# Attention of a diffusion block: value products in four column tiles, reciprocals spread by DMA, both heads' scores in float32r, inverse roots from Ln and Exp, GpSimd takes sums

## The chip, the cores and the metric

The kernel runs on one core of a Trainium2 chip. A core has TensorE (PE, matrix products; the loading of its stationary operand is shown as PEld), VectorE (DVE), ScalarE (ACT), GpSimd (POOL) and SyncE (SP, which here only issues DMA transfers). The on-chip memory SBUF has 128 partitions; TensorE writes its sums into PSUM, eight banks of 128 x 512 float32. Each engine runs its own instructions in order, and semaphores order the engines among themselves. The metric is device microseconds of one execution, as the median of several runs.

## The reference

Two layers of a diffusion transformer on 512 tokens of width 1024 with 256 tokens of context. Layer 0 mixes tokens by a Fourier transform and a long convolution, layer 1 by attention with low-rank queries, keys and values. Both end with a gated convolutional feed-forward. The change touches layer 1's attention and its output projection:

```python
def _rms_norm(x, g):
    y = x32 * lax.rsqrt(jnp.mean(x32 * x32, axis=-1, keepdims=True) + EPS)
    return (y * _f32(g)).astype(x.dtype)
...
q = (_rms_norm(a_q, q_a_norm) @ w_uq).reshape(B, L, MLA_HEADS, QK_HEAD_DIM)   # 16 heads of 64 + 32
q = _rms_norm(q, q_norm)                       # then the rotation of the last 32
...
k = _rms_norm(jnp.concatenate([k_nope, k_pe], axis=-1), k_norm)               # 512 + 256 keys
...
s = jnp.einsum('bqhd,bkhd->bhqk', qblk, k) * scale
p = jax.nn.softmax(s, axis=-1)
o = jnp.einsum('bhqk,bkhv->bqhv', p, v)        # value heads of 64
...
yx = o @ mla_w_o[j]
x = x + g1 * yx
```

## The kernel before

All weights and activations of the large products are kept as a float32r pair, a high part (a copy by ScalarE, `hi`, L240) and a residual (a subtraction by VectorE, `lo`, L245). `mm3` (L263 to L267) makes a product of three float32r products: high by high, high by residual, residual by high. Some products are plain float32 instead.

Attention runs over eight pairs of heads, `p` = 0 to 7. The heads of a pair are `a` = 0 and 1. Keys lie in six tiles `j` of 128 (four of tokens, two of context); the 512 queries are the free dimension. The scores therefore stand as keys x queries. The work of each pair is cut into small named steps, and the text `ORDER` (L36 to L66) lists all steps of all pairs in the order in which they are written out; TensorE, VectorE, ScalarE and GpSimd then run their own instructions in exactly that order. SyncE (the engine SP, not the step of that name) isn't held to it, but its queue is in order too. A step `SC13.5` is the step SC with a = 1, j = 3 of pair 5. The steps:

- QT, TB: products for the queries and their rotation; UK: key products, into the PSUM tile "k2"; SQ, RD, KSQ, KS: squares and their sums; TX: the rotation. KH and KL: high part and residual of the keys in SBUF. Only head 0 has a residual; head 1's keys are float32, in two alternating buffers.
- RT: the inverse roots of 20 columns of sums of squares, by `rsqrt` (L269 to L285): a start value from integer operations, then three Newton steps, 11 VectorE instructions, after two that form the means.
- U: scales the queries by these roots (four ScalarE instructions a head); TR: four transposes; QC and QL: high part and residual of the queries, QL for head 0 only.
- SC: a score tile 128 x 512. Head 0 by `mm3`, head 1 as one float32 product (L2019). EV: ScalarE copies it to SBUF, scaled by the key's root.
- MA, MB, MC, MD: VectorE's maximum over the six tiles. AR: GpSimd's maximum over the 128 partitions. SU: VectorE subtracts it, three tiles at a time. EX: ScalarE's Exp, three tiles at a time.
- PW: value products of one key tile (L2072), two matrix products with 64 columns of values each, one a head, in two column tiles of the array, into one "pv" bank. ON: the sums of the exponentials (L2083), four products with 32 columns of ones, in four column tiles, into the other "pv" bank. "pv" has two buffers.
- RC: reciprocal of the sums, 128 x 256, each row of which stands 32 times. TO: ScalarE copies the value products out of PSUM. SP: two TensorE products with a mask (L2098) that bring the reciprocals to the value rows' layout. DV: VectorE's product of both. OH, OL: high part and residual of the attention's output.
- VP, VE: the values of all heads, made on the way of the first pairs. WA/WD and XA/XD: splits of the query weights and of the output projection's weights, into the buffers "wh" and "wl" (three each, as "wr" for raw weights). WO m k: the output projection's block m of 128 columns with pair k's output.

Blocks 0 and 1 of the output projection are formed by WO within ORDER, in the attention's PSUM. The function `res_proj` does the other six, in two halves of 256 tokens; block 2's weights come split from the attention, those of the other blocks are loaded and split as they come (block 2's and 3's again for the second half). The residual is spilled to DRAM during attention and read back behind it.

Of the kernel before, what the change touches and what calls it, by code (L numbers as in the profile page):

```python
# [48 lines left out]
EV12.3 SC13.3 SU11.2 EX10.2 SC14.3 SC15.3 RT.4 EX11.2 ON0.2 PW0.2 EV13.3 ON1.2 MB0.3 KH0.4 PW1.2 U0.4 MC0.3 ON2.2 KL0.4 PW2.2 KH1.4 MD0.3 ON3.2 EV14.3
ON4.2 AR0.3 ON5.2 U1.4 MA1.3 PW3.2 PW4.2 EV15.3 RC.2 PW5.2 TR0.4 TO.2 SU00.3 QT.5 QC0.4 QL0.4 EX00.3 MB1.3 TR1.4 MC1.3 SQ.5 SP.2 TB.5 QC1.4 SC00.4  # L50
XA0.7 DV.2 SC01.4 TX.5 EV00.4 SC02.4 RD.5 EV01.4 SC03.4 MD1.3 EV02.4 SC04.4 SU01.3 EV03.4 AR1.3 UK.5 EV04.4 OH.2 SC10.4 XD0.7 KSQ.5 SC05.4 EV10.4
SC11.4 MA0.4 EV05.4 SC12.4 EX01.3 SU10.3 SC13.4 EV11.4 KS.5 SU11.3 EV12.4 EX10.3 SC14.4 RT.5 SC15.4 EX11.3 PW0.3 ON0.3 EV13.4 ON1.3 MB0.4 U0.5 PW1.3
MC0.4 ON2.3 OL.2 KH0.5 PW2.3 KH1.5 MD0.4 ON3.3 ON4.3 KL0.5 EV14.4 AR0.4 ON5.3 U1.5 PW3.3 MA1.4 PW4.3 EV15.4 RC.3 PW5.3 TR0.5 TO.3 SU00.4 QT.6 QC0.5
QL0.5 EX00.4 MB1.4 TR1.5 MC1.4 SC00.5 SQ.6 TB.6 SP.3 QC1.5 EV00.5 RD.6 SC01.5 SC02.5 TX.6 EV01.5 DV.3 SC03.5 EV02.5 MD1.4 SC04.5 OH.3 SU01.4 SC05.5
AR1.4 EV03.5 UK.6 EV04.5 EV05.5 OL.3 SC10.5 KSQ.6 SC11.5 MA0.5 EX01.4 SC12.5 SU10.4 EV10.5 KS.6 EV11.5 EV12.5 SU11.4 SC13.5 EX10.4 SC14.5 RT.6 SC15.5
EX11.4 ON0.4 ON1.4 EV13.5 PW0.4 MB0.5 EV14.5 ON2.4 U1.6 MC0.5 ON3.4 ON4.4 MA1.5 PW1.4 U0.6 PW2.4 MD0.5 KH0.6 MB1.5 ON5.4 AR0.5 PW3.4 KH1.6 RC.4 PW4.4
EV15.5 TR1.6 KL0.6 PW5.4 QC1.6 SU00.5 TR0.6 TO.4 QT.7 QC0.6 MC1.5 EX00.5 QL0.6 MD1.5 SC00.6 SU01.5 AR1.5 SQ.7 SP.4 EV00.6 SC01.6 XA1.7 TB.7 SC02.6
EV01.6 DV.4 SC03.6 EV02.6 TX.7 SC10.6 RD.7 EV03.6 SC04.6 EX01.5 SU10.5 UK.7 EV10.6 SC05.6 SU11.5 EV04.6 SC11.6 EV05.6 SC12.6 KSQ.7 XD1.7 SC13.6 EV11.6
EV12.6 MA0.6 KS.7 EX10.5 MB0.6 SC14.6 EX11.5 RT.7 SC15.6 ON0.5 EV13.6 ON1.5 PW0.5 EV14.6 MC0.6 U0.7 ON2.5 MA1.6 PW1.5 U1.7 PW2.5 MD0.6 MB1.6 ON3.5
AR0.6 KH0.7 ON4.5 ON5.5 KH1.7 KL0.7 PW3.5 EV15.6 RC.5 PW4.5 OH.4 PW5.5 XA2.7 SU00.6 TR0.7 TO.5 TR1.7 QC0.7 SP.5 QC1.7 QL0.7 WO00.7 EX00.6 MC1.6 SC00.7  # L60
SU01.6 SC01.7 EV00.7 SC02.7 EV01.7 SC03.7 MD1.6 EX01.6 SC04.7 OL.4 AR1.6 WO10.7 DV.5 EV02.7 WO01.7 EV03.7 XD2.7 SC10.7 EV04.7 OH.5 SC11.7 MA0.7 EV10.7
SC05.7 EV11.7 SU10.6 SC12.7 EV05.7 SC13.7 EV12.7 SU11.6 WO02.7 EX10.6 SC14.7 EV13.7 WO11.7 MB0.7 EX11.6 WO03.7 MC0.7 SC15.7 OL.5 EV14.7 WO12.7 MD0.7
EV15.7 ON0.6 MA1.7 AR0.7 PW0.6 ON1.6 MB1.7 ON2.6 PW1.6 MC1.7 ON3.6 MD1.7 ON4.6 SU00.7 PW2.6 AR1.7 ON5.6 PW3.6 RC.6 EX00.7 PW4.6 PW5.6 SU10.7 WO13.7
TO.6 WO04.7 SU01.7 EX10.7 WO14.7 SP.6 SU11.7 PW0.7 EX01.7 ON0.7 ON1.7 DV.6 EX11.7 PW1.7 ON2.7 PW2.7 OH.6 ON3.7 OL.6 ON4.7 ON5.7 PW3.7 RC.7 PW4.7 PW5.7
SP.7 TO.7 WO15.7 DV.7 WO05.7 OH.7 WO16.7 OL.7 WO06.7 WO07.7 WO17.7
"""  # L66
SPLIT = (0,)
# [119 lines left out]
class Builder:  # L187
# [1031 lines left out]
    def res_proj(self, i, sec, src_h, src_l, nk, wsrc, x, parts, hook=None, keep=None, ready=0, pre=None, there=False, ahead=None):  # L1219
# [7 lines left out]
        ws = dict(ahead or {})  # L1227

# [13 lines left out]
        for stage, part in enumerate(parts):  # L1242
            for j, m in enumerate(second if stage else range(KD)):
# [4 lines left out]
                if not (stage and (m >= KD - 3 or m < kept)) and not first and (stage or m not in ws):  # L1248
                    ws[m] = load(m)
                wh, wl = ws.get(m, (None, None))  # L1250
                ps = pre if first else self.mm()
                for k in range(0 if first else nk):
                    w = slice(128 * k, 128 * k + 128)
                    for a, n in part:
                        self.mm3(ps[:, a : a + n], wh[:, w], wl[:, w], src_h[k][:, a : a + n], src_l[k][:, a : a + n], k == 0, k == nk - 1)
# [467 lines left out]
    def attention(self, x, hh, hl, steps, aw):  # L1723
# [12 lines left out]

        K = [[self.t(pa, [P, TW], F32R if a in SPLIT else F32, f"K{a}{q}") for q in range(2)] for a in range(2)]
        keys = lambda p, a: K[a] if a in SPLIT else [K[a][p % 2]]
        tabm, tabx = self.t(pa, [P, 4, 192], F32, "tabm"), self.t(pa, [P, 4, 64], F32, "tabx")
        ssp = self.t(pa, [P, 20], F32, "ssp")  # L1740
        msk = self.t(pa, [P, 418], F32, "msk")
        rot, ksel, fan, ones = msk[0:64, 0:128], msk[:, 128:130], (msk[:, 130:258], msk[:, 258:386]), msk[:, 386:418]
# [53 lines left out]
        with self.tc.manual_schedule(engines={ENG.PE, ENG.DVE, ENG.Activation, ENG.Pool}):  # L1796
# [98 lines left out]
            rt, prot = MS(), [S1(), S1()]  # L1895
# [13 lines left out]
            def rotary_out():  # L1909
                v.memset(ssp, EPS)  # L1910
                v.tensor_scalar(ssp[:, 8:20].rearrange("p (a b) -> p a b", b=2), rt[:, 0:6].rearrange("p (a o) -> p a o", o=1).to_broadcast([P, 6, 2]),
                                1.0 / 96, EPS, op0=ALU.mult, op1=ALU.add)
                for a in range(2):
                    rows = slice(64, 128) if a == 0 else slice(0, 64)
                    for ps, (o, m) in zip(prot, sg):
                        self.hi(K[a][0][rows, o : o + m], ps[rows, :m])
                        if a in SPLIT:
                            self.lo(K[a][1][rows, o : o + m], ps[rows, :m], K[a][0][rows, o : o + m])
                    if a not in SPLIT:
                        nc.gpsimd.tensor_copy(K[a][1][rows, :], K[a][0][rows, :])  # L1920

# [46 lines left out]
            def KH(c, p, a):  # L1968
                rows = slice(0, 64) if a == 0 else slice(64, 128)
                self.hi(keys(p, a)[0][rows, :], c.k[rows, :TW])  # L1970
# [5 lines left out]
            def KS(c, p):  # L1976
                c.rt = MS()
                for j, t0 in enumerate(tok):
                    nc.tensor.matmul(c.rt[:, 2 * j : 2 * j + 2], c.ks[:, t0 : t0 + 128], ksel, start=True, stop=True)

            def RT(c, p):

                s = self.t(self.sm, [P, 24], F32, "nrm_s", 4)
                v.tensor_scalar(s[:, 0:8], c.s[:, 0:8], 1.0 / 96, EPS, op0=ALU.mult, op1=ALU.add)
                v.scalar_tensor_tensor(s[:, 8:20], c.rt[:, 0:12], 1.0 / 96, ssp[:, 8:20], op0=ALU.mult, op1=ALU.add)
                c.r = self.t(pq, [P, 24], F32, "rks", 3)
                self.rsqrt(self.sm, s, 20, c.r)

            def U(c, p, a):
                for t_ in range(4):  # L1990
                    q = c.t[:, t_, 128 * a : 128 * a + 128]
                    nc.scalar.activation(q, q, AF.Copy, scale=c.r[:, 2 * t_ + a : 2 * t_ + a + 1])
# [8 lines left out]
            def QC(c, p, a):  # L2001
                if not hasattr(c, "qT"):
                    c.qT, c.S, c.m, c.P, c.Z, c.ps = {}, {}, {}, None, None, {}
                q = self.t(pq, [P, T], F32R if a in SPLIT else F32, f"q{a}")
# [8 lines left out]
            def SC(c, p, a, j):  # L2013
                ps = c.ps[a, j] = S1()
                k_, q = [t_[:, tok[j] : tok[j] + 128] for t_ in keys(p, a)], c.qT[a]
                if a in SPLIT:
                    self.mm3(ps, *k_, *q, True, True)
                else:
# [672 lines left out]
```

## Time and profile before

| | |
|---|---|
| median of three runs | 1561.67 us (1561.05 to 1565.24) |
| the profiled execution | 1566.02 us |
| its span in the trace | 1564.3 us |
| mean granted TensorE clock | 0.991 |
| the listed order in that span, about | 954 to 1172 us |
| output projection behind it, about | 1172 to 1210 us |

The profile is one execution. A timeline row has start, duration, engine, line of the kernel, operation, result <- operands by the program's names, shape and count; matrix products are pipelined, so that durations overlap and the distance between starts is what one costs. A row of costly groups has busy time and mean duration in ns, then the idle time ahead of the group and what ended it. A row by windows has busy microseconds and instructions of each engine in a stretch, the granted clock and the DMA engines' share. A row of transfers has the issuing queue, count, KB each and the median time from issue to landing.

### The profile page before, as it was taken

The page shows a single profiled execution, that of the slowest core. Times are in us where ns is not written, and L with a number is a line of the kernel's source. Part 1 is how long each engine was busy: PE and PEld are TensorE (multiplying, and loading weights), DVE is VectorE, ACT ScalarE, POOL GpSimd, SP SyncE. Part 2 cuts the span into 40 slices and gives each one's busy share as a digit, 9 for nine tenths or more (in the row PEclk, how much of TensorE's full clock was granted, in tenths as well). Part 3 has the DMA queues.
Part 4 walks back from the last instruction along what each step waited for, and adds up shares of the span by engine and source line. Part 5 has one row for each costly group of instructions (what it writes and reads, how often), then busy time and mean ns, then how long its engine had stood idle before and what let it go on. Part 6 is the DMA issues. An engine that isn't in the chain of part 4 may idle for free.

```text
span 1564.3 us, 24106 instructions
## 1 busy us (share of the span) xinstructions
PE 1519.6 (97%) x9192; PEld 1310.9 (84%) x9192; DVE 1284.0 (82%) x2197; ACT 748.5 (48%) x1130; POOL 255.8 (16%) x407
## 2 busy tenths in 40 slices
PE   7999998999999999999999999999999999999998
PEld 5687888888999999999889887656559999989997
DVE  5788969968997997886769767899877999878884
ACT  4451224426543444443334337988855555434442
POOL 0013125201011112111111000112130021212100
PEclk9999998999999999999999999999999999999999
DMA  9336512536267778788686711000044365656543
GB/s 351 114 108 205 184 67 68 175 136 210 74 168 191 190 189 199 186 213 218 175 210 192 268 53 44 14 14 15 14 117 133 95 164 160 157 142 160 143 111 105
DMA packets 84513, 224.17 MB, mean 143 GB/s; under 512 B 10283, under 2 KB 16621, under 8 KB 83373
## 3 DMA queue, kind: packets, MB, share of 16 engines
q1 hardware_dynamic: 60205, 161.72, 31.3%
q0 software_dynamic: 24192, 60.91, 18.8%
q8 instruction: 72, 1.18, 0.3%
q14 instruction: 44, 0.36, 0.1%
HBM read 201.01 MB, written 21.58 MB: 142 GB/s over the span
## 4 chain that ended last, share of the span: by engine, by line
PE 72%; DVE 13%; DMA 8%; issue 3%; ACT 3%; POOL 1%; SPq 0%; ACTq 0%; DVEq 0%; POOLq 0%
PE mm L265 16%; PE mm L266 16%; PE mm L267 16%; DMA sb<-wmodT 3%; DVE junk L347 3%; PE pv L2072 3%; PE s L2019 3%; PE ms L265 3%; PE ms L266 3%; PE ms L267 3%; DVE wl L245 2%; DMA sb<-w_up 2%; PE pv L2083 2%; ACT wh L240 1%; PE k L266 1%
## 5 line engine op out<-in xcount | busy, mean ns | idle before, releaser
L240 ACT ACTIVATE wh<-wr 128x1024 fp32r<-128x1024 f32 (+3 forms) x182 | 158.1, 878 | 199.4 <-PE mm L266 120.8
L265 PE MATMUL mm<-hh,wh 128*128 128x512 f32 (+3 forms) x704 | 232.5, 330 | 2.1 <-DVE xr L1343 1.5
L266 PE MATMUL mm<-hl,wh 128*128 128x512 f32 (+3 forms) x704 | 230.4, 327 | 2.4 <-DVE hl L424 2.3
L267 PE MATMUL mm<-hh,wl 128*128 128x512 f32 (+3 forms) x704 | 229.8, 326 | 2.3 <-DVE wl L245 2.3
L245 DVE TENSOR_TENSOR wl<-wr,wh 128x1024 fp32r<-128x1024 f32 (+3 forms) x182 | 184.4, 1018 | 16.4 <-ACT wh L240 16.0
L265 PEld LDWEIGHTS mm<-hh,wh 128*128 128x128 f32 x704 | 134.7, 191 | 14.3 <-issue 4.7
L266 PEld LDWEIGHTS mm<-hl,wh 128*128 128x128 f32 x704 | 134.5, 191 | 11.8 <-DVE hl L424 3.3
L267 PEld LDWEIGHTS mm<-hh,wl 128*128 128x128 f32 x704 | 134.0, 190 | 12.1 <-DVE wl L245 4.5
L347 DVE SCALAR_TENSOR_TENSOR junk<-wr,sb 128x1024 bf16<-128x1024 f32 x96 | 117.2, 1221 | 4.2 <-DMA wr<-wmodT 4.1
L265 PE MATMUL ms<-hh,wh 128*128 128x386 f32 (+2 forms) x240 | 76.3, 318 | 1.1 <-DVE fg L1527 1.1
L266 PE MATMUL ms<-hl,wh 128*128 128x386 f32 (+2 forms) x240 | 76.3, 318 | 0.0
L267 PE MATMUL ms<-hh,wl 128*128 128x386 f32 (+2 forms) x240 | 76.3, 318 | 0.0
L267 PE MATMUL mm<-x,wl 128*128 128x512 f32 (+1 forms) x224 | 75.9, 339 | 0.3 <-DVE wl L245 0.3
L266 PE MATMUL mm<-x,wh 128*128 128x512 f32 (+1 forms) x224 | 76.0, 339 | 0.0
L265 PE MATMUL mm<-x,wh 128*128 128x512 f32 (+1 forms) x224 | 76.0, 340 | 0.0
L265 PE MATMUL mm<-ah,wh 128*128 128x512 f32 x176 | 69.7, 396 | 0.0
L266 PE MATMUL mm<-al,wh 128*128 128x512 f32 x176 | 69.7, 396 | 0.0
L267 PE MATMUL mm<-ah,wl 128*128 128x512 f32 x176 | 69.7, 396 | 0.0
L2027 ACT ACTIVATE S<-s,rks 128x512 f32<-128x512 f32 x96 | 62.8, 686 | 3.8 <-PE s L267 1.9
L2044 POOL PARTITION_ALL_REDUCE mx<-mx x16 | 38.2, 2385 | 158.6 <-DVE mx L2041 140.7
L2278 POOL DMA_DIRECT2D sum<-w_up x40 | 23.4, 601 | 234.8 <-DVE wl L245 160.4
L240 ACT ACTIVATE wh<-sum 128x1024 fp32r<-128x1024 f32 x40 | 42.3, 1058 | 36.0 <-PE mm L266 14.5
(514 smaller groups left out, 4521.2 us busy)
## 6 DMA issues: line engine op xcount, KB each, us to landing
wr<-wmodT SPq DMA_DIRECT2D x48, 512.0 KB, 4.1
wr<-w_up SPq DMA_DIRECT2D x48, 512.0 KB, 4.0
sum<-w_up POOLq DMA_DIRECT2D x80, 256.0 KB, 4.4
sb<-wmodT SPq DMA_DIRECT2D x32, 512.0 KB, 4.8
xs<-delta POOLq DMA_DIRECT2D x32, 386.0 KB, 6.5
wr<-w_dn SPq DMA_DIRECT2D x48, 256.0 KB, 3.8
sa<-w_up POOLq DMA_DIRECT2D x40, 256.0 KB, 4.3
sb<-w_up POOLq DMA_DIRECT2D x40, 256.0 KB, 5.1
```

Of the source, the lines that this page charges most:

```text
L240: self.nc.scalar.activation(dst, src, AF.Copy)
L245: (eng or self.nc.vector).tensor_tensor(dst, src, hi.bitcast(F32), op=ALU.subtract)
L265: mmul(out, wh, xh, start=start, stop=False)
L266: mmul(out, wh, xl, start=False, stop=False)
L267: mmul(out, wl, xh, start=False, stop=stop)
L347: nc.vector.scalar_tensor_tensor(junk, raw, 1.0, self.sb[j], op0=ALU.mult, op1=ALU.mult, accum_out=acc)
L2019: nc.tensor.matmul(ps, k_[0], q[0], start=True, stop=True)
L2027: nc.scalar.activation(c.S[a][j // 3][:, j % 3, :], c.ps[a, j], AF.Copy, scale=c.r[:, g : g + 1])
L2044: nc.gpsimd.partition_all_reduce(c.m[a][:, 1, :], c.m[a][:, 0, :], P, bass.bass_isa.ReduceOp.max)
L2072: nc.tensor.matmul(c.P[64 * a : 64 * a + 64, :], V[:, j, o : o + 64], c.S[a][j // 3][:, j % 3, :], start=c.np == 0, stop=c.np == 5, tile_p ...
L2083: nc.tensor.matmul(c.Z[o : o + 32, 0:256], ones, c.S[a][j // 3][:, j % 3, 256 * h : 256 * h + 256], start=c.nz == 0, stop=c.nz == 5, tile_ ...
L2278: nc.gpsimd.dma_start(t_[:, 512:1024], g[:, 0:512])
```

## The change

1. PW: four products of 32 value columns in four column tiles, instead of two of 64. In the new ORDER, PW and ON stand together more often.
2. Head 1's scores by `mm3` as well. So there are KL1 and QL1; keys have one buffer (high part, residual) for each head.
3. RC's input is first copied (ZC) and sent over DRAM (ZA, two transfers: four rows of 256 out, 128 x 8 in), so that the reciprocal works on 128 x 8; ZB sends it back to DRAM and ZD's two transfers read it as rows spread over 64 partitions each. TO and SP go; DV multiplies the value products in PSUM directly.
4. RT in three steps: NA (the two means' instructions), NB (ScalarE: Ln, then Exp with the factor -0.5), RT (one Newton step, three instructions). One table load stands ahead of ORDER.
5. GpSimd subtracts the maximum for one key tile in six (SV; the second SU has two tiles) and forms OL.
6. U of head 0 is one VectorE product with a broadcast operand. MB and MC become one operation of two tiles. A head's scores stand in one buffer of six tiles (four buffers) instead of two of three (eight).
7. Block 2 of the output projection is done in ORDER too (eight more WO), and block 3's weights are split there into buffers of the query part (LX3, XA3, XD3); `res_proj` starts at block 3 and keeps these weights for the second half. Loads of raw weights are steps of their own (LW, LX).
8. In PSUM, "s" has four buffers instead of three, and "ms" goes.

ORDER is new as a whole. Its stretch around pair 3's value products before:

```
EX11.3 PW0.3 ON0.3 EV13.4 ON1.3 MB0.4 U0.5 PW1.3 MC0.4 ON2.3 OL.2 KH0.5 PW2.3 KH1.5 MD0.4 ON3.3 ON4.3 KL0.5 EV14.4 AR0.4 ON5.3
U1.5 PW3.3 MA1.4 PW4.3 EV15.4 RC.3 PW5.3 TR0.5 TO.3 SU00.4 QT.6 QC0.5 QL0.5 EX00.4 MB1.4 TR1.5 MC1.4 SC00.5 SQ.6 TB.6 SP.3 QC1.5
EV00.5 RD.6 SC01.5 SC02.5 TX.6 EV01.5 DV.3
```

and after:

```
PW0.3 NB.5 AR0.4 ON0.3 EV13.4 RT.5 PW1.3 KH0.5 MA1.4 ON1.3 U1.5 ON2.3 PW2.3 U0.5 KL0.5 KH1.5 PW3.3 SV0.4 EV14.4 SU00.4 ON3.3 ON4.3
EV15.4 PW4.3 OH.2 KL1.5 PW5.3 EX00.4 OL.2 ON5.3 MB1.4 TR1.5 ZC.3 TR0.5 XA1.7 ZA.3 SU01.4 QT.6 QC0.5 MD1.4 QC1.5 EX01.4 QL0.5 AR1.4
QL1.5 SC00.5 TB.6 SQ.6 SC10.5 SC11.5 EV00.5 RC.3 TX.6 ZB.3 EV10.5 RD.6 SC01.5 SV1.4 EV11.5 UK.6 SU10.4 EV01.5 SC02.5 KSQ.6 ZD.3
SC12.5 SU11.4 EV02.5 SC03.5 EV12.5 SC04.5 XD1.7 EV03.5 SC05.5 EV04.5 MA0.5 KS.6 LX0.7 EV05.5 EX10.4 DV.3
```

The core of the diff:

```diff
-            S1 = lambda: self.t(psB, [P, 512], F32, "s", 3)
-            MS = lambda: self.t(psB, [P, 512], F32, "ms", 1)
+            S1 = lambda: self.t(psB, [P, 512], F32, "s", 4)
...
+            def NB(c, p):
+                a = self.t(self.sm, [P, 24], F32, "rq_a", 1)
+                nc.scalar.activation(a[:, :20], c.n[:, :20], AF.Ln)
+                c.g = self.t(self.sm, [P, 24], F32, "rq_r")
+                nc.scalar.activation(c.g[:, :20], a[:, :20], AF.Exp, scale=-0.5)
+
             def RT(c, p):
...
+                g, b = c.g[:, :20], self.t(self.sm, [P, 24], F32, "rq_b", 1)
+                v.tensor_tensor(b[:, :20], g, g, op=ALU.mult)
+                v.scalar_tensor_tensor(b[:, :20], b[:, :20], -0.5, c.n[:, :20], op0=ALU.mult, op1=ALU.mult)
                 c.r = self.t(pq, [P, 24], F32, "rks", 3)
-                self.rsqrt(self.sm, s, 20, c.r)
+                v.scalar_tensor_tensor(c.r[:, :20], b[:, :20], 1.5, g, op0=ALU.add, op1=ALU.mult)
...
-                if a in SPLIT:
-                    self.mm3(ps, *k_, *q, True, True)
-                else:
-                    nc.tensor.matmul(ps, k_[0], q[0], start=True, stop=True)
+                self.mm3(ps, *k_, *q, True, True)
...
             def SU(c, p, a, h):
+                n = 3 - h
                 mb = c.m[a][:, 1, :].rearrange("p (o q) -> p o q", o=1)
-                v.tensor_tensor(c.S[a][h], c.S[a][h], mb.to_broadcast([P, 3, T]), op=ALU.subtract)
+                s = c.S[a][:, 3 * h : 3 * h + n, :]
+                v.tensor_tensor(s, s, mb.to_broadcast([P, n, T]), op=ALU.subtract)
+
+            def SV(c, p, a):
+                s = c.S[a][:, 5, :]
+                nc.gpsimd.tensor_tensor(s, s, c.m[a][:, 1, :], op=ALU.subtract)
...
             def PW(c, p, j):
...
                 for a in range(2):
-                    o = 128 * p + 64 * a
-                    nc.tensor.matmul(c.P[64 * a : 64 * a + 64, :], V[:, j, o : o + 64], c.S[a][j // 3][:, j % 3, :], start=c.np == 0, stop=c.np == 5,
-                                     tile_position=(0, 64 * a))
+                    for u in range(2):
+                        r = 64 * a + 32 * u
+                        nc.tensor.matmul(c.P[r : r + 32, :], V[:, j, 128 * p + r : 128 * p + r + 32], c.S[a][:, j, :], start=c.np == 0, stop=c.np == 5,
+                                         tile_position=(0, r))
...
-            def TO(c, p):
+            def ZC(c, p):
+                c.z = self.t(pq, [P, 256], F32, "z")
+                nc.scalar.copy(c.z, c.Z[:, 0:256])
+
+            def ZA(c, p):
+                c.zd = [self.t(dr, [4, 256], F32, f"zd{i}", 2) for i in range(2)]
+                c.zr = self.t(pq, [P, 8], F32, "zr")
+                nc.sync.dma_start(c.zd[0], c.z[0:128:32, :])
+                nc.sync.dma_start(c.zr, c.zd[0].rearrange("g (r f) -> (g r) f", f=8))
+
+            def RC(c, p):
+                v.reciprocal(c.zr, c.zr)
+
+            def ZB(c, p):
+                nc.sync.dma_start(c.zd[1].rearrange("g (r f) -> (g r) f", f=8), c.zr)
+
+            def ZD(c, p):
+                c.R = self.t(pq, [P, T], F32, "R")
+                for a in range(2):
+                    nc.sync.dma_start(c.R[64 * a : 64 * a + 64, :], c.zd[1][2 * a : 2 * a + 2, :].rearrange("h f -> (h f)").partition_broadcast(64))
+
+            def DV(c, p):
                 c.O = self.t(pq, [P, T], F32, "O", 2)
-                nc.scalar.copy(c.O, c.P)
...
-            def SP(c, p):
-                c.R = MS()
-                for h in range(2):
-                    nc.tensor.matmul(c.R[:, 256 * h : 256 * h + 256], fan[h], c.z, start=True, stop=True)
-
-            def DV(c, p):
-                v.tensor_tensor(c.O, c.O, c.R, op=ALU.mult)
+                v.tensor_tensor(c.O, c.P, c.R, op=ALU.mult)
...
-                self.lo(Ol[p], c.O, Oh[p])
+                self.lo(Ol[p], c.O, Oh[p], nc.gpsimd)
...
-            Sp = self.pool("Sp", bufs=8)
+            Sp = self.pool("Sp", bufs=4)
+            nc.scalar.add_instruction(mybir.InstLoadActFuncSet(name=nc.get_next_instruction_name(), engine=mybir.EngineType.Activation, act_func_set_id=6))
...
-        self.res_proj(1, 2, oh, ol, KD, lambda m: I["w_o"][m], x, half, whook, ready=2, ahead=w2)
+        self.res_proj(1, 2, oh, ol, KD, lambda m: I["w_o"][m], x, half, whook, ready=3, ahead=w2)
```

More of the change, by code (lines that the diff above doesn't have):

```diff
@@ L1247, in res_proj @@
                 first = pre is not None and stage == 0 and m == 0
-                if not (stage and (m >= KD - 3 or m < kept)) and not first and (stage or m not in ws):
+                if not (stage and (m >= KD - 3 or m < kept)) and not first and (m not in held if stage else m not in ws):
                     ws[m] = load(m)
@@ L1735, in attention @@
         qal = [self.t(pa, [P, T], F32R, f"qal{k}") for k in range(2)]
-        K = [[self.t(pa, [P, TW], F32R if a in SPLIT else F32, f"K{a}{q}") for q in range(2)] for a in range(2)]
-        keys = lambda p, a: K[a] if a in SPLIT else [K[a][p % 2]]
+        K = [[self.t(pa, [P, TW], F32R, f"K{a}{q}") for q in range(2)] for a in range(2)]
         tabm, tabx = self.t(pa, [P, 4, 192], F32, "tabm"), self.t(pa, [P, 4, 64], F32, "tabx")
         ssp = self.t(pa, [P, 20], F32, "ssp")
-        msk = self.t(pa, [P, 418], F32, "msk")
-        rot, ksel, fan, ones = msk[0:64, 0:128], msk[:, 128:130], (msk[:, 130:258], msk[:, 258:386]), msk[:, 386:418]
+        msk = self.t(pa, [P, 162], F32, "msk")
+        rot, ksel, ones = msk[0:64, 0:128], msk[:, 128:130], msk[:, 130:162]
         pt = self.pool("pt", bufs=2, side="right")
@@ L1969, in KH @@
                 rows = slice(0, 64) if a == 0 else slice(64, 128)
-                self.hi(keys(p, a)[0][rows, :], c.k[rows, :TW])
+                self.hi(K[a][0][rows, :], c.k[rows, :TW])
             def KL(c, p, a):
@@ L2173, in layer1 @@
             nc.sync.dma_start(x[d], xd[d])
-        for m in range(2):
-            nc.vector.scalar_tensor_tensor(x[m], pre[:, 512 * m : 512 * m + 512], self.mod[1][:, 16 + m, 0:1], x[m], op0=ALU.mult, op1=ALU.add)
+        for m in range(3):
+            nc.vector.scalar_tensor_tensor(x[m], pre[m], self.mod[1][:, 16 + m, 0:1], x[m], op0=ALU.mult, op1=ALU.add)
         self.close("psB")
@@ L2578, in constants @@
     c["ropeK"] = rk
-    am = np.zeros((P, 418))
+    am = np.zeros((P, 162))
     r_, j_ = np.arange(64)[:, None] % 32, np.arange(32)[None, :]
@@ L2584, in constants @@
     am[64:, 129] = 1.0
-    for a in range(2):
-        for h in range(2):
-            am[32 * (2 * a + h), 130 + 128 * h + 64 * a : 194 + 128 * h + 64 * a] = 1.0
-    am[:, 386:418] = 1.0
+    am[:, 130:162] = 1.0
     c["amsk"] = am
```

156 lines of the change are left out of this document (84 added, 72 removed).

## The prediction

> **What bounds the kernel now.** I read the page's head first, then the busy times of the attention alone, then TensorE's order of time in one head pair.
>
> ```profile
> span 1564.3 us, 24106 instructions
> PE 1519.6 (97%) x9192; PEld 1310.9 (84%) x9192; DVE 1284.0 (82%) x2197; ACT 748.5 (48%) x1130; POOL 255.8 (16%) x407
> PE 72%; DVE 13%; DMA 8%; issue 3%; ACT 3%; POOL 1%; SPq 0%; ACTq 0%; DVEq 0%; POOLq 0%
> ...
> core 0: us, PE busy (x) PEld busy (x) DVE busy (x) ACT busy (x) POOL busy (x), PEclk, DMA share, GB/s
> 957.00:1172.00 215.00, 214.60 (x1287) 127.24 (x1287) 183.34 (x272) 172.44 (x266) 43.98 (x24) 1.00 0.11 33
> ```
>
> The edit lies in the attention, 957 to 1172 us, and in the output projection behind it. There TensorE (PE) is busy 214.6 of 215 us at full clock: it waits for nothing, and of the chain that ended last 72% is TensorE's. VectorE (DVE) has 183 us of work, 85%, ScalarE (ACT) 172, 80%. So the time falls only by what leaves TensorE, and rises by any wait that the fuller order cannot hide.
>
> One pair, by starts on TensorE:
>
> ```profile
> 1038.87 0.39 PE L265 MATMUL s<-q,K 128*128 128x512 f32 x1
> ...
> 1039.56 2.74 PE L2019 MATMUL s<-q,K 128*128 128x512 f32 x6
> 1042.13 1.40 PE L1979 MATMUL ms<-msk,sq 128*128 128x2 f32 x12
> ...
> 1046.14 0.64 PE L2083 MATMUL pv<-S,msk 128*32 128x256 f32 x8
> 1046.71 1.08 PE L2072 MATMUL pv<-S,V 128*64 128x512 f32 x4
> 1047.72 0.64 PE L2083 MATMUL pv<-S,msk 128*32 128x256 f32 x8
> ...
> 1050.88 1.50 PE L2083 MATMUL pv<-S,msk 128*32 128x256 f32 x24
> 1052.31 2.79 PE L2072 MATMUL pv<-S,V 128*64 128x512 f32 x12
> 1055.03 0.66 PE L1999 MATMUL s<-cst,t 128*128 128x128 f32 x4
> ...
> 1058.62 1.03 PE L2098 MATMUL ms<-z,msk 128*128 128x256 f32 x4
> 1059.30 0.58 PE L265 MATMUL s<-q,K 128*128 128x512 f32 x1
> 1059.72 0.39 PE L266 MATMUL s<-ql,K 128*128 128x512 f32 x1
> ```
>
> Prices are start to start, since ends overlap. A split score (L265, L266, L267) takes 1039.56 - 1038.87 = 0.69 us, 0.23 a product. A plain f32 score takes (1042.13 - 1039.56)/3 = 0.857.
>
> **The change on TensorE.** *Scores.* 48 scores of head 1 go from 0.857 to 0.69: 48 x 0.16 = -7.7 us. *The step SP.* From 1058.62 to 1059.30 is 0.68, and the next product's step is 0.42 instead of 0.23, so 0.86 in all with rounding: 8 x 0.86 = -6.9.
>
> *Value products.* One set alone costs 1.01 (1046.71 to 1047.72), three cost 2.72 (1052.31 to 1055.03): 0.857 a set and 0.15 a run. Sums: one set 0.57, three 1.43: 0.43 a set and 0.14 a run. A set of sums streams 4 x 256 columns in half the time in which a set of values streams 2 x 512; so four tiles of 32 columns really run side by side, and PW in four tiles of 512 should again cost 0.86. What can fall is the fixed part. Counting stretches of PW alone and ON alone the old order has 56; in the new one both have the same tiling and stand together in 16 stretches. If the fixed part belongs to the change of tiling, 40 x 0.145 = -5.8; if to any change between PW and ON (49 stretches), 7 x 0.145 = -1.0. A run of sums costs as much before values as behind them, so I take the tiling, -5.8.
>
> *Output projection.* Eight more products WO, each 0.69, enter attention: +5.5. What they replace:
>
> ```profile
> 1172.20:1210.00 37.80, 35.83 (x297) 35.53 (x296) 30.30 (x64) 20.59 (x41) 0.00 (x0) 0.96 0.40 129
> L267 PE MATMUL mm<-Oh,wl 128*128 128x256 f32 x96 | 27.6, 287 | 2.0 <-DVE wl L245 2.0
> ```
>
> 35.8 us for six blocks of weights in two halves: 6.0 a block, so -0.5 net. The 2.0 us of idle wait for split weights; three of the splits go (block 2's reload, block 3's load and reload). I take -1, between -2 and +4, as the residual's and the weights' loads stand behind the last spreading transfers on SP.
>
> The sum on TensorE is -7.7 - 6.9 - 5.8 - 0.5 - 1 = -21.9.
>
> **The change on VectorE.**
>
> ```profile
> L2048 DVE TENSOR_TENSOR S<-S,mx 128x1536 f32<-128x1536 f32 x32 | 54.8, 1738 | 0.0
> L2093 DVE RECIPROCAL z<-pv 128x256 f32<-128x256 f32 x8 | 14.0, 1753 | 6.2 <-PE pv L2083 6.2
> L245 DVE TENSOR_TENSOR K<-k,K 64x772 fp32r<-64x772 f32 x7 | 6.6, 942 | 3.3 <-ACT K L240 3.3
> L245 DVE TENSOR_TENSOR ql<-s,q 128x512 fp32r<-128x512 f32 x7 | 4.8, 682 | 1.1 <-ACT q L240 1.1
> L245 DVE TENSOR_TENSOR Ol<-O,Oh x8: 683/693/1530, 1014.2 to 1169.7; 128x512 fp32r<-128x512 f32 x8
> 1045.27 0.18 DVE L274 TENSOR_SCALAR rq_i<-nrm_s 128x20 int32<-128x20 int32 x1
> ...
> 1047.40 0.18 DVE L283 SCALAR_TENSOR_TENSOR rks<-rq_b,rq_r 128x20 f32<-128x20 f32 x1
> 1047.50 0.68 DVE L2035 TENSOR_TENSOR mx<-mx,S 128x512 f32<-128x512 f32 x1
> ```
>
> The inverse root is 11 small operations from 1045.27 to 1047.50, 2.2 us; three stay, 0.6: -13 over eight pairs. The reciprocal falls from 1.75 to that of 8 columns, at most a small operation, 0.2: -12.4. OL leaves, 8 x 0.69 or more: -6. SU of the second half loses one tile of three, 16 x 0.53 (a third of 1.738, less a fixed part): -8.5. Added: KL of head 1 8 x 0.94 = 7.5, QL 5.5, U of head 0 8 x 0.68 = 5.5. In all 183 - 40 + 18.5 = 162 of some 200 us, 81%.
>
> GpSimd takes 24 new operations; what they do to VectorE has a bound:
>
> ```profile
> L2044 POOL PARTITION_ALL_REDUCE mx<-mx x16 | 38.2, 2385 | 158.6 <-DVE mx L2041 140.7 <-PE s L2019 17.9
> L1043 POOL TENSOR_TENSOR sx<-sx,sx x12: 1266/1297/2284, 228.1 to 265.7; 128x512 f32<-128x512 f32 x12
> ```
>
> GpSimd's 128x512 sum takes 1.27 to 2.28 us, and OL's subtraction on VectorE 0.68 to 1.53: the extremes are what either pays when the other is at work, +0.85 to +1.0. Each of 24 could hold VectorE by 0 to 0.85: 0 to 20 us, VectorE 162 to 182, 81 to 91%. Before, 85% cost TensorE nothing, so up to there it is hidden; I take half and price it at +1 of TensorE's waits. GpSimd itself has 2 x 2.4 + 3 x 1.3 = 8.7 us of 22 per pair.
>
> The Trainium skill's page "SBUF — State Buffer", section "Who interferes with whom", speaks against this edit: a VectorE operation with both inputs in SBUF and a GpSimd operation that reads SBUF take turns on a shared port, the later one blocked until the first is done. By it the 24 could cost VectorE their whole 1.27 us, an estimate of 30 us, and VectorE would stand at 96%; the 0.85 above is the most that a row here shows.
>
> **ScalarE.**
>
> ```profile
> L1992 ACT ACTIVATE t<-t,rks 128x128 f32<-128x128 f32 x56 | 17.5, 391 | 0.4 <-DVE rks L283 0.4
> L2089 ACT COPY O<-pv 128x512 f32<-128x512 f32 x8 | 4.7, 587 | 18.6 <-PE pv L2072 18.6
> L2051 ACT ACT_TABLE_LOAD x1 | 1.3, 1283 | 0.0
> ```
>
> Half of the single-block U's gone, some -10 to -12; TO -4.7; ZC, half of TO's columns, 8 x 0.3 to 0.59; Ln and Exp, 16 x 0.2 to 0.39. About 165 of 200 us, hidden as before. One table load, 1.28 us, stands ahead of the order, and head 1's keys get a residual there: at most +2.5, against the first root's -1.6: I take +0.5.
>
> **The reciprocal's way over DMA.** This is the new wait. Behind the last ON come ZC, two transfers, RC, one transfer, two broadcasts at once, DV: four transfers in a row, all in the in-order queue of the engine SP. The trace has no such transfer in this place; the nearest rows:
>
> ```profile
> cT<-cT SPq DMA_DIRECT2D x1, 8.0 KB, 2.3
> cst<-cst SPq DMA_DIRECT2D x1, 66.0 KB, 2.1
> Hd<-s SPq DMA_DIRECT2D x6, 256.0 KB, 2.6
> s<-Hd SPq DMA_DIRECT2D x6, 256.0 KB, 5.2
> gg<-gq SPq DMA_DIRECT2D x1, 128.0 KB, 4.2
> ```
>
> Three carry 4 KB: 2.1 to 2.3. The broadcast has the shape of gg, a row to many partitions, which SP issues behind the rotation's tables: 2.1 to 4.2. With ZC 0.4, RC 0.2 and issue 0.3 the quotient can start 9.5 to 12.0 us after the sums, DV's 0.68 comes on top: 10 to 12.7. At 0.69 a score and the prices above, the new order gives TensorE 15.1, 10.0, 10.0, 11.7, 9.5, 10.6 and 10.7 us of products between ZC and DV of pairs 0 to 6, and 1.0, 1.7, 1.7, 2.1, 4.6, 0.4 and 1.3 more until the next pair needs the accumulator that DV frees ("pv" has two buffers). So it is covered up to 11.0 to 16.1 us, 12.9 in the mean. At 10 us nothing shows, at 12.7 (1.7 + 1.0 + 1.0 + 0.7 lacking in four pairs) 4.4 us. Behind DV in VectorE's order stand MD, MB and KL, so a late DV makes the next scores late as well. I take +3, for the last pair +1.5 (12.8 us of products stand there behind its last sums, against 10 to 12.7 us and then OH and OL). Several of those bounds are wide: 0 to +14 together.
>
> **The sum.** -21.9 + 0.5 + 1 + 3 + 1.5 = -15.9. The profiled run took 1566.0 us, 1564.3 of span and 1.7 around it; its own time becomes 1550.1. It lies 4.3 over the median of the runs, 1561.67, which becomes 1545.8, say 1546.
>
> **The rivals.**
>
> *VectorE becomes the bound* through GpSimd's new operations. For it: 91% at the upper price, and an order in which SV stands between AR and EX. Against: the median OL stayed at 0.69 beside GpSimd's reductions of 2.4 us. Eight pairs lose about 1 us each: 1554.
>
> *No wait at all*: transfers at 2.1 us and free ports. For it: in the attention TensorE idles 0.4 of 215 us today. -15.9 less 5.5 gives 1540 to 1541.
>
> *The transfers are late.* Write and read back as in Hd and s cost 2.6 + 5.2, twice, 15.6 us for the four instead of 8.8: the quotient comes 17.2 us behind the sums. Lacking in pairs 0 to 6: 1.1, 5.5, 5.5, 3.4, 3.1, 6.2, 5.2, together 30 us: slower than before, 1546 - 4 + 30 = 1572. It eats the whole gain from about 3.5 us a transfer. For it: loads on the same queue. Against: those were 256 KB each, and the DMA engines' share here is 0.11.
>
> *Ln and Exp in different tables*: two loads of 1.28 us a pair, 20.5 us on ScalarE, which would stand at 185 of 200: 1552. The Trainium skill's page "ScalarE: Activation LUTs", section "Table sets: the hidden batching unit", names one set that has both, with one load; no run shows it yet.
>
> *Four tiles don't run side by side* with 512 columns: 48 x 0.86 = +41, 1587. The sums' row speaks against it.
>
> **How the numbers follow.** Forecast 0.52 (own range 1541 to 1552), VectorE 0.22, no wait 0.10, late transfers 0.09, tables 0.04, tiles 0.03. The time is the forecast's, 1546. The range 1538 to 1558 takes in the first three and the tables and leaves late transfers and tiles out, with some of VectorE's tail: 0.19. A measurement of this kernel tells 0.3%, 4.7 us, from no change: faster means below 1557. That is 0.52 + 0.10 + 0.04 + 0.19 of VectorE's 0.22: 0.85. Within it: the rest of VectorE's and a little of the transfers', 0.05; slower 0.10.
>
> **What the profile after would show.** No L2019 f32 score and no fan products; attention about 200 us of TensorE work; PW sets 0.86 apart, no step where ON follows PW; 96 scores at 0.69. DV's start minus its pair's last sum is 10 to 12.7 us if the transfers are as priced. Waits of TensorE for DV show late transfers, waits for EV or EX behind SU and SV show VectorE. One table load, not sixteen. Wrong would be: a PW set over 1 us, a transfer over 3.5 us, or VectorE above 95% in attention.

## The result, and the profile after

| | before | after |
|---|---|---|
| median | 1562.86 us (1561.05 to 1565.24) | 1651.15 us (1644.36 to 1662.87) |
| ratio of the runs | | 1.057, 95% interval 1.051 to 1.064 |
| span of the profiled execution | 1564.3 us | 1642.3 us |
| granted TensorE clock, whole span | 0.991 | 0.966 |

The changed kernel is 88 us slower. The forecast was 16 us faster, and 1651 lies above every rival's time. The profile's page of the changed kernel opens so:

```profile
span 1642.3 us, 24552 instructions
PE 1534.7 (93%) x9376; PEld 1328.6 (81%) x9376; DVE 1263.2 (77%) x2133; ACT 739.6 (45%) x1113; POOL 278.4 (17%) x430
```

No engine but GpSimd (17% where it had 16%) is fuller than before. The work by engine in the attention, from 957 us to the first product of the output projection's function (1255.27 here, 1172.22 before; columns as in the prediction):

```profile
957.00:1255.27 298.27, 233.78 (x1511) 149.71 (x1511) 165.03 (x208) 164.14 (x250) 60.51 (x40) 0.86 0.09 28
```

The attention takes 83 us longer. TensorE waits for 64.5 us of it, and its work takes 233.8 us, where it took 214.6 before and the forecast had it fall; the granted clock there is 0.86, it was 1.00. VectorE has 165 us of work (162 were foretold) and ScalarE 164 (165 foretold), both in 298 us. All four engines wait. The waits of the same kernel, by engine, what the waiting instruction was, its releaser, the total in us, how often, and the longest:

```profile
POOL S L2057 <- issue: 77.8, 11, 7.3
...
ACT S L2061 <- POOL S L2057: 63.3, 12, 20.6
DVE S L2053 <- POOL mx L2047: 57.6, 15, 11.8
...
POOL mx L2047 <- issue: 36.4, 6, 6.5
PE pv L2094 <- ACT S L2061: 35.7, 7, 20.3
```

Read from the bottom: TensorE's sums wait for ScalarE's Exp, Exp waits for GpSimd's subtraction, VectorE for GpSimd's reduction. At the top GpSimd waits for nothing that the profile can name ("issue"), and always for 6 to 7 us. Its order of time, with the idle time ahead of each instruction in brackets:

```profile
1006.76 1.80 POOL L2047 PARTITION_ALL_REDUCE mx<-mx  x1 [6.04 <-DVE K L246]
1015.89 1.29 POOL L2057 TENSOR_TENSOR S<-S,mx 128x512 f32<-128x512 f32 x1 [7.33 <-issue]
1023.12 1.80 POOL L2047 PARTITION_ALL_REDUCE mx<-mx  x1 [5.94 <-DVE mx L2038]
1032.22 1.27 POOL L2057 TENSOR_TENSOR S<-S,mx 128x512 f32<-128x512 f32 x1 [7.30 <-issue]
1039.48 1.80 POOL L2047 PARTITION_ALL_REDUCE mx<-mx  x1 [5.99 <-DVE K L246]
1048.45 1.27 POOL L2057 TENSOR_TENSOR S<-S,mx 128x512 f32<-128x512 f32 x1 [7.17 <-issue]
1049.69 1.28 POOL L246 TENSOR_TENSOR Ol<-O,Oh 128x512 fp32r<-128x512 f32 x1
```

Over the whole attention each turn from the reduction to an ordinary sum leaves 6.8 to 7.3 us empty, 7.1 in the mean, and each turn back 5.7 to 6.5, 6.0 in the mean. OL directly behind SV pays nothing: it is the turn that costs, not the sum. The last column names VectorE instructions for some of the turns back; the gap stays the same whoever is named, so that name is a coincidence. One head takes 1.8 + 7.1 + 1.3 + 6.0 = 16.2 us, two heads 32.7 (1006.76 to 1039.48), where the forecast counted on 22 us a pair. What happens in the gaps stands among the instructions by line, of the changed kernel's reduction and SV:

```profile
L2047 POOLq MODIFY_POOL_CONFIG  x32: 1/1/13, 904.8 to 1216.7; - x32
...
L2057 POOLq MODIFY_POOL_CONFIG  x30: 98/98/98, 976.2 to 1224.1; - x30
```

and of the kernel before:

```profile
L2044 POOL PARTITION_ALL_REDUCE mx<-mx x16: 1782/2079/3147, 973.8 to 1149.5; - x16
L2044 POOLq MODIFY_POOL_CONFIG  x2: 4/6/9, 956.1 to 956.2; - x2
```

These instructions come in pairs, one pair a turn. From their name I read that the engine is given other code, and call it an exchange of code; what the trace itself shows is the pair and the gap behind it. The old kernel turned once to the reductions, at 956 us, 17 us before it needed the first; the new one does it some 30 times in the attention. The instruction itself is over in 0.1 us or less, isn't counted as busy, and the cost stands nowhere but in the gap behind it.

**Theory L**: this exchange of code paces the attention. Its rivals: **P**, GpSimd's sums block VectorE's port; **D**, the reciprocal's way over DMA holds DV; **S**, it is the sums' size and waits.

### The profile page after: what moved, and what is told of

Read it like the earlier page. It is cut to its first block, busy times and chain, and to the rows that moved or that the text cites. A ratio compares the mean times of both kernels' runs of the same rounds, so it can differ in the third digit from the quotient of the medians.

```text
span 1642.3 us, 24552 instructions
## 1 busy us (share of the span) xinstructions
PE 1534.7 (93%) x9376; PEld 1328.6 (81%) x9376; DVE 1263.2 (77%) x2133; ACT 739.6 (45%) x1113; POOL 278.4 (17%) x430
## 5 line engine op out<-in xcount | busy, mean ns | idle before, releaser
L246 DVE TENSOR_TENSOR wl<-wr,wh 128x1024 fp32r<-128x1024 f32 (+3 forms) x179 | 180.2, 1012 | 16.3 <-ACT wh L241 15.5
L2053 DVE TENSOR_TENSOR S<-S,mx 128x1536 f32<-128x1536 f32 (+1 forms) x32 | 47.0, 1488 | 57.7 <-POOL mx L2047 57.6
L2061 ACT ACTIVATE S<-S 128x1536 f32<-128x1536 f32 x32 | 47.3, 1484 | 96.7 <-POOL S L2057 63.3
L2094 PE MATMUL pv<-S,msk 128*32 128x256 f32 x384 | 37.7, 448 | 35.7 <-ACT S L2061 35.7
```

Source lines behind the costliest of these rows:

```text
L246: (eng or self.nc.vector).tensor_tensor(dst, src, hi.bitcast(F32), op=ALU.subtract)
L2053: v.tensor_tensor(s, s, mb.to_broadcast([P, n, T]), op=ALU.subtract)
L2061: nc.scalar.activation(s, s, AF.Exp)
L2094: nc.tensor.matmul(c.Z[o : o + 32, 0:256], ones, c.S[a][:, j, 256 * h : 256 * h + 256], start=c.nz == 0, stop=c.nz == 5, tile_position=(0, o))
```

## The experiments

Where a line of the code is changed, the numbers of lines in the fences are those of that kernel.

**The sums on VectorE again.**

```diff
-                nc.gpsimd.tensor_tensor(s, s, c.m[a][:, 1, :], op=ALU.subtract)
+                v.tensor_tensor(s, s, c.m[a][:, 1, :], op=ALU.subtract)
...
-                self.lo(Ol[p], c.O, Oh[p], nc.gpsimd)
+                self.lo(Ol[p], c.O, Oh[p])
```

> The changed kernel, with SV and OL on VectorE again (same places in ORDER); GpSimd keeps only the 16 reductions. Theory L (GpSimd exchanges its code at each turn between the reduction and an ordinary operation, 5.9 to 7.3 us of idle each, 33 such turns in place of 2, which makes 16.1 us a head or 32 us a pair and sets the pace): the gaps go, VectorE gets 16 x 0.6 + 8 x 0.7 = 15 us more, 177 of about 200 us; TensorE sets the pace again, the time is 1543 to 1553 us. Rival D (the reciprocal's way over DMA holds DV and with it the accumulators): it stays slow, above 1600 us. Rival P (GpSimd's sums block VectorE's port): also 1543 to 1553, so this run alone doesn't tell P from L.

Measured: 1551.59 us, ratio to before 0.990 (0.986 to 0.994). Two lines are worth 0.067 of the time. Its attention by engine, and one pair's way of the reciprocal:

```profile
957.00:1164.37 207.37, 204.79 (x1515) 137.22 (x1514) 178.38 (x232) 162.74 (x249) 33.31 (x16) 0.99 0.12 40
```

```profile
1051.56 0.37 ACT L2100 COPY z<-pv 128x256 f32<-128x256 f32 x1
1051.95 0.52 SPq L2105 DMA_DIRECT2D zd<-z  x1
1053.57 0.32 SPq L2106 DMA_DIRECT2D zr<-zd  x1
1056.37 0.19 DVE L2109 RECIPROCAL zr<-zr 128x8 f32<-128x8 f32 x1
1056.59 0.33 SPq L2112 DMA_DIRECT2D zd<-zr  x1
1058.07 1.10 SPq L2117 DMA_DIRECT2D R<-zd  x2
```

TensorE is full again, at a clock of 0.99: 204.8 us of work where the changed kernel shows 233.8, and 2.6 us of idle where it shows 64.5. So of the 91 us between both attentions 62 are waits and 29 the same products at a lower clock. D falls: the whole way over DMA is still in this kernel.

**Reductions replaced by ordinary copies.** GpSimd keeps its 24 sums and gets 16 copies, so that no turn to a reduction is left: the trace shows no MODIFY_POOL_CONFIG on the lines of the copies and of SV. The kernel leaves out the maximum over the partitions.

```diff
-                nc.gpsimd.partition_all_reduce(c.m[a][:, 1, :], c.m[a][:, 0, :], P, bass.bass_isa.ReduceOp.max)
+                nc.gpsimd.tensor_copy(c.m[a][:, 1, :], c.m[a][:, 0, :])
```

> The changed kernel with GpSimd's reduction over partitions replaced by an ordinary GpSimd copy of the same 128x512 tile (the maximum over the partitions is left out, each partition subtracts its own); the 24 GpSimd sums stay, and 16 copies beside them. Theory L: no exchange of code is left after the start, so no gaps of 6 to 7 us; 1543 to 1556 us. Rival P (the port): 40 ordinary GpSimd operations block VectorE as before or more; it stays above 1600 us. Rival D: above 1600 us.

Measured: 1554.41 us, 0.994 (0.990 to 0.997). P falls, and with it S as far as the sums' size goes: 40 GpSimd operations without a turn between kinds cost no TensorE time that can be told from the run above. What they do cost VectorE shows against the kernel with the sums on VectorE. First that one, then this:

```profile
L2053 DVE TENSOR_TENSOR S<-S,mx 128x1536 f32<-128x1536 f32 x16 | 27.9, 1746 | 0.1
L2041 DVE TENSOR_TENSOR mx<-mx,S 128x1024 f32<-128x1024 f32 x16 | 20.2, 1260 | 0.7 <-ACT S L2034 0.5
```

```profile
L2053 DVE TENSOR_TENSOR S<-S,mx 128x1536 f32<-128x1536 f32 x16 | 29.0, 1812 | 0.1
L2041 DVE TENSOR_TENSOR mx<-mx,S 128x1024 f32<-128x1024 f32 x16 | 21.9, 1369 | 0.8 <-ACT S L2034 0.5
```

1.1 and 1.7 us more over 16 operations each, and others grew as well. In all VectorE has 175 us of work in this attention; the run above has 178, of which SV and OL are 16, so its other operations take 162 there. They cost 13 us more beside GpSimd's 40, within the 0 to 20 us bound of the prediction. Giving GpSimd these sums thus takes only some 3 us off VectorE in the end.

**Only OL on GpSimd.** OL stays where the change put it.

```diff
-                nc.gpsimd.tensor_tensor(s, s, c.m[a][:, 1, :], op=ALU.subtract)
+                v.tensor_tensor(s, s, c.m[a][:, 1, :], op=ALU.subtract)
```

> The changed kernel with SV on VectorE, OL still on GpSimd: two exchanges a pair instead of four. Theory L: GpSimd needs 1.8 x 2 + 7.1 + 1.3 + 5.9 = 17.9 us a pair, under TensorE's 22.5, so the pace is TensorE's, but a reduction that falls behind an exchange comes up to 14 us late; 1548 to 1580 us. Rival P: two thirds of the port's loss gone, a third left: some 1580 us. Rival D: above 1600 us.

Measured: 1581.55 us, 1.010 (1.006 to 1.013), 1.5 us over the range of theory L. GpSimd isn't full, so it is the lateness of a reduction behind two exchanges that counts: in the trace VectorE's subtraction SU waits for the reduction three times, 19.2 us in all. P's number is met as well (1580), but P is out by the run before.

**One part alone, in the kernel before: SV.**

```diff
-                v.tensor_tensor(c.S[a][h], c.S[a][h], mb.to_broadcast([P, 3, T]), op=ALU.subtract)
+                n = 3 - h
+                s = c.S[a][h][:, 0:n, :]
+                v.tensor_tensor(s, s, mb.to_broadcast([P, n, T]), op=ALU.subtract)
+
+            def SV(c, p, a):
+                s = c.S[a][1][:, 2, :]
+                nc.gpsimd.tensor_tensor(s, s, c.m[a][:, 1, :], op=ALU.subtract)
```

> The kernel before with one part of the change alone: GpSimd subtracts the maximum for one key tile in six (SV right behind each AR), VectorE's second SU has two tiles. Theory L: 16 reductions and 16 sums alternate, 32 exchanges; 16.1 us a head, 32 us a pair where the pair took 25, so 1562 + 8 x 7 = about 1615 us (1600 to 1630). Rival P: at most 16 x 1.3 us more on VectorE, which has 32 us to spare: 1558 to 1575 us. Rival D: no change, 1555 to 1565 us.

Measured: 1639.88 us, 1.047 (1.042 to 1.051): none of the rest of the change is needed for the loss. It is 10 us over the expected range. The expectation took no account of the clock, and here, too, TensorE was granted less (the attention of this kernel, and the first 4 us of the output projection, which begins at 1241.00):

```profile
957.00:1245.00 288.00, 242.20 (x1314) 135.01 (x1315) 179.54 (x268) 172.66 (x268) 60.09 (x40) 0.92 0.08 25
```

Without those 4 us it is 238 us of TensorE work for products that take 215 in the kernel before.

**A dummy behind the reduction.** The first run's kernel, plus an ordinary sum of 128x8 behind each reduction, which nobody waits for.

```diff
+                d = self.t(pq, [P, 8], F32, "dum", 2)
+                nc.gpsimd.tensor_tensor(d, ssp[:, 8:16], ssp[:, 8:16], op=ALU.add)
```

> The run with the sums on VectorE, and behind each reduction an ordinary GpSimd sum of 128x8 that nobody waits for. Theory L: 32 exchanges again, 1.8 + 7.1 + 0.1 + 5.9 = 14.9 us a head, 29.8 us a pair against 22.5: 8 x 7.3 = 58 us more than without, 1590 to 1625 us. Rival S (the size of the sums, their port and their waits made the loss): no change, 1548 to 1554 us.

Measured: 1621.22 us, 1.037 (1.035 to 1.039). Its instructions on that line, and GpSimd's order of time:

```profile
L2049 POOLq MODIFY_POOL_CONFIG  x32: 98/98/98, 979.5 to 1208.2; - x32
```

```profile
1032.47 0.32 POOL L2049 TENSOR_TENSOR dum<-ssp 128x8 f32<-128x8 f32 x1 [6.99 <-DVE nrm_s L1981]
1038.97 1.80 POOL L2047 PARTITION_ALL_REDUCE mx<-mx  x1 [6.19 <-issue]
1048.08 0.19 POOL L2049 TENSOR_TENSOR dum<-ssp 128x8 f32<-128x8 f32 x1 [7.30 <-issue]
```

This settles L against S: 16 sums with a median of 0.25 us, with no reader and hardly any data, cost some 70 us, because each brings a turn and a turn back.

**Value products in four tiles alone, in the kernel before.** The old ORDER stays.

```diff
-                    o = 128 * p + 64 * a
-                    nc.tensor.matmul(c.P[64 * a : 64 * a + 64, :], V[:, j, o : o + 64], c.S[a][j // 3][:, j % 3, :], ...
+                    for u in range(2):
+                        r = 64 * a + 32 * u
+                        nc.tensor.matmul(c.P[r : r + 32, :], V[:, j, 128 * p + r : 128 * p + r + 32], c.S[a][j // 3][:, j % 3, :], ...
```

> The kernel before with the value products alone in four tiles of 32 columns, in the old ORDER. If the fixed 0.145 us belongs to the change of tiling, 56 stretches become 9: 47 x 0.145 = 6.8 us less on TensorE, 0.4%, ratio 0.9957. If every turn between PW and ON costs it, no change (1.000). If four tiles of 512 columns don't run side by side: 41 us more, 1.026.

Measured: 1557.60 us, 0.9964 (0.9949 to 0.9979); the expected 0.9957 lies within. TensorE in order:

```profile
1048.50 1.04 PE L2073 MATMUL pv<-S,V 128*32 128x512 f32 x8
1049.36 1.48 PE L2084 MATMUL pv<-S,msk 128*32 128x256 f32 x24
1050.65 2.76 PE L2073 MATMUL pv<-S,V 128*32 128x512 f32 x24
```

One set of values 0.86, three sums 1.29 = 3 x 0.43, with nothing fixed on top: between two kinds of the same tiling the turn is free.

**Head 1 in float32 again**, in the first run's kernel (KL1 and QL1 do nothing, keys and queries of head 1 are float32).

```diff
-                self.mm3(ps, *k_, *q, True, True)
+                if a:
+                    nc.tensor.matmul(ps, k_[0], q[0], start=True, stop=True)
+                else:
+                    self.mm3(ps, *k_, *q, True, True)
```

> As the run with the sums on VectorE, but head 1's scores, keys and queries in float32 again (no KL1, no QL1). If TensorE sets the pace: 48 x 0.16 = 7.7 us more than that run, 1557 to 1561 us. If VectorE does: 13 us of its work go, and the time falls to 1540 to 1550 us.

Measured: 1553.94 us, 0.9943 (0.9922 to 0.9963). In absolute terms it misses both ranges. Against the kernel before, whose own median moved between 1562.5 and 1565.5 us from one set of runs to the next, it is 0.0043, 6.7 us, worse than the first run's kernel, near the 7.7 of TensorE's side; as the intervals overlap, its size isn't certain. Nor is it the price of the scores alone, for the same edit takes 13 us off VectorE.

**Two more transfers** between the sums and the reciprocal, in the first run's kernel.

```diff
+                nc.sync.dma_start(c.zd[2].rearrange("g (r f) -> (g r) f", f=8), z1)
+                nc.sync.dma_start(c.zr, c.zd[2].rearrange("g (r f) -> (g r) f", f=8))
```

> The run with the sums on VectorE, and two more transfers (to DRAM and back, 4 KB each, some 3.5 us together) between the sums and the reciprocal, which doubles neither work nor code exchanges. If the way over DMA is at the edge of its cover (11.3 us from ZC to DV, cover 12.9 in the mean with DV): 15 us more, 1560 to 1572 us. If it is hidden with room: 1549 to 1554 us.

Measured: 1568.12 us, 1.0015 (1.000 to 1.003), 17 us more than without. So the way over DMA is covered for the most part, and there is no room for more: two 4 KB transfers a pair take back the whole gain. The waits on VectorE show where (total in us, how often, longest):

```profile
DVE zr L2112 <- DMA zr<-zd: 19.4, 7, 6.3
```

In the first run's kernel the same wait is 3.2 us, once, and DV waits 7.5 us, in four pieces, for the broadcast rows.

**The last three** ask what bounds the first run's kernel, where VectorE is busy for 97% of a steady stretch and TensorE for 99%:

```profile
980.00:1100.00 120.00, 118.85 (x933) 80.60 (x932) 115.87 (x150) 103.84 (x161) 20.16 (x11) 1.00 0.08 23
```

One subtraction of three tiles instead of SV and a shorter SU (SV does nothing):

```diff
-                n = 3 - h
+                n = 3
```

> The run with the sums on VectorE, and SV put back into SU: three tiles in one operation of 1.75 us instead of two tiles in 1.27 and one in 0.68, 16 x 0.2 = 3 us less on VectorE. TensorE sets the pace: no change against that run, ratio to before 0.988 to 0.991. VectorE (busy 29 of 30 us in a steady stretch of it) sets the pace: 2 to 3 us less.

The old inverse root on VectorE (NB does nothing):

```diff
-                v.tensor_tensor(b[:, :20], g, g, op=ALU.mult)
...
+                self.rsqrt(self.sm, c.n, 20, c.r)
```

> The run with the sums on VectorE, with the eleven-step inverse root on VectorE in place of Ln, Exp and one step: 8 x 1.7 = 13 us more VectorE work. If VectorE has room behind TensorE: 1549 to 1555 us. If it is at its end already: 8 to 13 us more, 1559 to 1566 us.

One subtraction, and U of head 0 on ScalarE:

```diff
-                if a:
+                if True:
                     for t_ in range(4):
-                        q = c.t[:, t_, 128:256]
-                        nc.scalar.activation(q, q, AF.Copy, scale=c.r[:, 2 * t_ + 1 : 2 * t_ + 2])
+                        q = c.t[:, t_, 128 * a : 128 * a + 128]
+                        nc.scalar.activation(q, q, AF.Copy, scale=c.r[:, 2 * t_ + a : 2 * t_ + a + 1])
```

> As the run with one subtraction, and U of head 0 back in four ScalarE operations: 8 x 0.69 = 5.5 us less on VectorE, 8 x 1.3 = 10 us more on ScalarE (88% busy in a steady stretch). TensorE sets the pace: no change, ratio 0.988 to 0.991. VectorE sets it: 3 to 6 us less. ScalarE takes over: 3 to 8 us more.

Measured, on one chip: 0.9955 (0.9942 to 0.9968), 1.0036 (1.0019 to 1.0053) and 0.9926 (0.9909 to 0.9943). The old root's own base is the first run's kernel, and against its 0.990 it costs 0.0136, 21 us, more than the 13 us of extra work and more than either forecast. So this work isn't hidden; but its trace also shows ScalarE's part of U waiting for the root eight times, 15.1 us in all (1.0 in the first run's kernel), so that a full VectorE and a root that comes later aren't told apart. Taking 5.5 us off VectorE gains 4.5 us against the one-subtraction kernel, within the 3 to 6 foretold. But the last kernel has some 8 us less VectorE work than the first run's and is not shown to be faster. The one-subtraction kernel itself came out worse than either forecast for it, with one run of 1546 and five of 1555 to 1557; why isn't settled. What bounds the first run's kernel therefore stays open between VectorE and TensorE. So does which of the faster ones is best: the first run's (0.990) and the last one's (0.993) overlap. Both beat the kernel before and the changed one.

## Why the prediction was wrong, point by point

**GpSimd.** The step that failed is the sentence "GpSimd itself has 2 x 2.4 + 3 x 1.3 = 8.7 us of 22 per pair". It added up the durations of the rows and took a turn between two kinds of instructions as free. The runs show four turns a pair at 6.0 and 7.1 us in the mean: 26 us more, and two heads in 32.7 us where TensorE needs 22.5 a pair in the first run's kernel. The row was in the trace of before, two instructions of under 0.01 us at 956 us; I hadn't asked what stood between a reduction and another operation, since all 16 reductions there followed one another. The page "GPSIMD Engine Reference" of the Trainium skill, section "2.1 Instruction dispatch", says that the first call of freshly loaded code also pays about 6 us, without an instruction that shows it. The trace agrees for the turn to the reduction, 6.0 us in the mean, and shows 7.1 for the turn to ordinary sums. Had every turn been priced by that sentence, 32 turns would have made an estimate of 190 us of GpSimd's time, and the forecast a slower kernel; that every turn pays is what the runs show, and not what the sentence says.

**The port**, which I had as the main risk on GpSimd, priced at +1 and as a rival at +8, cost VectorE 13 us of work beside 40 GpSimd operations, and TensorE nothing that can be told. The prediction's argument that the median OL stayed at 0.69 us beside the reductions didn't hold: the three OLs of 1.53 us in the trace of before (1014.21, 1039.08 and 1089.25 us) are those that ran during a reduction.

**TensorE's sum came out near, in part by luck.** With the sums on VectorE the attention ends at 1164.37 instead of 1172.22, 7.9 us earlier; foretold were -20.4 + 5.5 + 0.5 + 1 + 3 + 1.5 = -8.9. But the parts miss: TensorE's work there fell by 9.8 us (214.6 to 204.8) and not by 14.9, and its idle time rose by 2.2 and not by 6, and the two misses nearly cancel. Behind it the span has 385.0 us instead of 392.1, 7.1 less; foretold were -5.5 - 0.5 - 1 = -7.0. In all it is 0.990, and 1546/1562 = 0.990 was forecast, though for a kernel with these sums on GpSimd. The scores in float32r are worth 6.7 of 7.7 us as far as that run can tell, the tiling 0.36% of 0.44%, and it is a change of tiling that costs, as I had chosen.

**The transfers.** Foretold were 2.1 to 2.3 us for the small ones and 2.1 to 4.2 for the broadcast. In the changed kernel, from issue to landing:

```profile
R<-zd SPq DMA_DIRECT2D x16, 128.0 KB, 3.3
...
zr<-zd SPq DMA_DIRECT2D x8, 4.0 KB, 1.5
zd<-zr SPq DMA_DIRECT2D x8, 4.0 KB, 1.9
```

That is inside or below; the cover of 12.9 us in the mean fits as well, since the two transfers more cost 17 us where 15 were expected from it.

**VectorE** was sized rightly (162 us foretold, 165 measured) and read too kindly. With the sums given back it stands at 178 of 207 us over the whole attention but at 97% in the middle, above the 95% that the prediction named as a sign of being wrong, and the old root's run shows that more work there isn't hidden. The average over the stage hid it.

**Tables.** The changed kernel loads a table once ahead of ORDER, and none within it:

```profile
L2187 ACT ACT_TABLE_LOAD x1 | 1.3, 1283 | 0.0
```

Ln, Exp and the copies share it; that rival falls.

## What to carry to other kernels

Before an engine gets work of another kind, look for what it does between kinds: one row of the new operation priced alone says nothing of it, and an engine that is busy for 20% of a stage can pace it by its turns alone. Run a cheap operation of the new kind beside the old one, with no reader, and look at the gaps. And where a bound engine is made to wait, count its products again: at a lower granted clock the same work took a seventh longer.

## What the runs showed of the hardware that was not expected

GpSimd's exchange of code takes 5.7 to 7.3 us each way in the changed kernel, shown only as idle time behind an instruction of 0.1 us or less. It is paid at every turn, not once for each kind of code.

TensorE's granted clock falls behind longer waits. In the changed kernel's attention, 22% idle, it is 0.86 in the mean. TensorE does nothing from 999 to 1002 us there, the clock is 0.50 from 1002 to 1005, and from 1008 it is 1.00 again; behind 1.9 us of idle time between 1116 and 1119 us it stays at 1.00. How long a wait it takes isn't shown. At 0.50 float32r products run at about half their pace: 0.43 us from start to start here, and 0.23 in the kernel before and a little later in the same kernel, at 1.00.

```profile
1049.28 0.63 PE L268 MATMUL s<-q,K 128*128 128x512 f32 x1
1049.70 0.63 PE L266 MATMUL s<-q,K 128*128 128x512 f32 x1
1050.13 0.63 PE L267 MATMUL s<-ql,K 128*128 128x512 f32 x1
...
1053.37 0.40 PE L266 MATMUL s<-q,K 128*128 128x512 f32 x1
1053.60 0.39 PE L267 MATMUL s<-ql,K 128*128 128x512 f32 x1
```

The lower clock makes 29 of the 91 us by which the changed kernel's attention is longer than the first run's.
